# Score tiles of two PSUM banks for pairs of heads in a decoder step on one Trainium2 core

## The chip, the cores and the metric

The kernel runs on one core of a Trainium2 chip. The metric is the device time of one execution in microseconds (us), lower is better. TensorE is called PE below, VectorE DVE, ScalarE ACT, GpSimd POOL.

## The reference

The program is one step of a small hybrid decoder on 256 prompt tokens and 8 sample tokens (264 columns in all): an S5 layer with a gated projection, a squared-ReLU MLP, a sparse-attention layer with three branches (compressed, selected, window), and a second MLP. The attention of the prompt is, for each of 16 query heads over 4 key heads and a causal mask:

```python
s_s = einsum('bqgrd,bqgkld->bqgrkl', qg, ks)       # selected keys
p_s = _masked_softmax(s_s, sel_mask)
o_s = einsum('bqgrm,bqgmd->bqgrd', p_s, vs)
s_w = einsum('bqgrd,blgd->bqgrl', qg, kw)          # window keys
p_w = _masked_softmax(s_w, w_mask)
o_w = einsum('bqgrl,blgd->bqgrd', p_w, vw)
o = g[..., 0:1] * o_c + g[..., 1:2] * o_s + g[..., 2:3] * o_w
```

`o_c` is the same over 8 compressed blocks. With 256 tokens every causal block is selected, so both large branches are plain causal attention over 256 keys, each with keys and values of its own.

## The kernel before, in words

Activations lie feature-major, 128 features by 264 tokens. A dense product (`mm3`, L597 to L599) is three fp32r matmuls into one accumulator: high half of the weights by high half of the activations, high by low, low by high. The weights come by DMA into `raw` (four buffers) and `wsplit` makes the halves: ACT writes `wh` (L590), DVE subtracts and writes `wl` (L591).

The stages follow one another: S5 to about 127 us, gated projection and first MLP to 364, keys, values, gates and queries to 440, attention to 528, its output projection to about 552, second MLP to the end. The order of the S5 stage is written by hand (`tc.manual_schedule()`, L1484); that of everything else is set by the scheduler of the TileContext (L1725), engine by engine, from the program, the buffers of each pool and its own estimates. Each engine then runs its list in order.

The end of the S5 stage: `down(1, 8, 8)` multiplies and adds the last carries into the states `St` on DVE (L454, L455), `from_states` (L471) multiplies them on PE for feature tiles 6 and 7, and the gated projection begins. A `wl` of that projection's weights that the list puts between is run between. `filler` runs pieces of the sample's compression in the gaps of this stage.

PSUM has eight banks of 128x512 f32; a tile asked for with `K.ps(tag)` is one bank of a tag's buffers. Before, tags `fl` (2) and `tr` (3) live through the program, `mm` (3) until the first MLP is done, then `sc` (2) and `po` (1); from there on `mm` is another name for `fl`.

Keys on their way: `kv_post` (L950 on) brings a branch's keys token-major with four transposes (`token_major`, L934), norms and rotates them (`norm_rope`, L987 to L998, on ACT, DVE and POOL, with `rsqrt_bits` L128 to L137 in small steps on DVE), and turns them back into `KTp` (`feature_major`, L944, copy L945). `q_post` does it for queries into `QT`. The queries of head groups 0 and 1 (`gp` 0) are made before the attention begins, those of `gp` 1 partly beside it (`Q1`, and generator `side_a`).

Attention (`prompt_attn`) takes 12 units `(gp, rp, u)`, each for two head groups `g2`, whose queries and keys lie in partitions 0 to 63 and 64 to 127, one PSUM bank per `g2`. Unit `u` 0 has the first 128 tokens of two heads per group: a mask matmul over the whole bank (L1187), then score matmuls of 256 columns (L1191). Units `u` 1 and 2 have the other 128 tokens of one head: one score matmul of 512 columns per bank (L1195), then a mask matmul of 256 columns (L1198). Each f32 matmul with 64 partitions shows as passes in the trace. `softmax` takes the negated row maximum (L1212, DVE), exponentials with sums (L1214, ACT, 4 or 2 per bank), and the scale (L1215 to L1223). `transposed` turns the result with four transposes per bank (L1232), `values` multiplies with the values (L1246, L1253). The loop issues scores of unit i, softmax of unit i-1, transposes and values of unit i-2, then `side(i)`: as many steps as `SIDE[i]` of the remaining queries and the compressed branch (`cmp_branch`, L1156 on), and as `SIDB[i]` of the sample tokens' attention (`sample_qk`, `sample_attn`).

## Time and profile before

| what | value |
|---|---|
| runs | 742.78, 740.6, 740.55 us |
| median | 740.6 us |
| profiled execution | 741.12 us |
| its span | 739.3 us |
| mean granted PE clock | 0.975 of full speed |
| PE busy | 700.2 us (95%) |
| DVE busy | 531.7 us (72%) |
| ACT busy | 404.6 us (55%) |
| POOL busy | 74.8 us (10%) |

The span is the stretch from the first to the last instruction, 1.8 us shorter than the profiled execution's own time. Busy shares are averages over stages that differ, so they are read by stage in windows. A timeline lists the instructions of one engine in order with their start, and in brackets the idle time before one and what ended it. Durations of matmuls overlap the next one; the distance from start to start is what one costs.

### The profile page before, as it was taken

What the parts mean: (1) busy time and instruction counts of PE and PEld (TensorE: products, weight loads), DVE (VectorE), ACT (ScalarE), POOL (GpSimd) and SP (SyncE); (2) the same over time, 40 slices, a digit from 0 to 9 for tenths busy, and PEclk for the clock granted to TensorE, in tenths of its full rate; (3) what the DMA queues carried; (4) which work ended last, traced back from release to release, by engine and by line L of the source; (5) the groups of instructions that cost most, each with busy time, mean ns of one, the idle gap of its engine ahead of it and who ended that gap; (6) DMA issues with size and microseconds to landing.
All of it is one profiled execution on the core that took longest, in us unless ns stands there. A gap on an engine that the chain in (4) does not pass through costs nothing.

```text
span 739.3 us, 16322 instructions
## 1 busy us (share of the span) xinstructions
PE 700.2 (95%) x6214; PEld 650.7 (88%) x6214; DVE 531.7 (72%) x1209; ACT 404.6 (55%) x907; POOL 74.8 (10%) x127
## 2 busy tenths in 40 slices
PE   2789897999999999999998999999999999999997
PEld 2787777999999999999988984565899999999997
DVE  7899995978777766656677868887678777755553
ACT  3463532666666655445466575657466666644442
POOL 0000623111000000000002224110020000000000
PEclk9989897999999999999999996999999999999999
DMA  7342423686767758555555564100255555556551
GB/s 263 81 158 77 161 99 118 197 289 193 229 234 262 277 175 298 186 175 188 177 175 179 188 187 142 59 3 1 86 172 182 188 173 182 189 180 201 192 190 40
DMA packets 53328, 124.70 MB, mean 169 GB/s; under 512 B 6522, under 2 KB 26874, under 8 KB 52994
## 3 DMA queue, kind: packets, MB, share of 16 engines
q1 hardware_dynamic: 51714, 121.23, 49.9%
q10 hardware_dynamic: 1536, 2.42, 0.9%
q8 instruction: 49, 0.80, 0.5%
q14 instruction: 29, 0.24, 0.1%
HBM read 120.63 MB, written 7.18 MB: 173 GB/s over the span
## 4 chain that ended last, share of the span: by engine, by line
PE 83%; DVE 13%; ACT 2%; issue 1%; DMA 1%; SPq 0%; ACTq 0%; DVEq 0%
PE ps_mm L597 23%; PE ps_mm L598 22%; PE ps_mm L599 22%; PE ps_sc L1195 3%; PE ps_tr L296 2%; PE ps_tr L1232 2%; PE ps_po L1253 2%; DVE ca L431 1%; DVE St L434 1%; DVE St L433 1%; DVE cb L432 1%; DVE St L455 1%; DMA U<-x_chunks_in 1%; DVE big L454 1%; PE ps_sc L1198 1%
## 5 line engine op out<-in xcount | busy, mean ns | idle before, releaser
L591 DVE TENSOR_TENSOR wl<-raw,wh 128x512 fp32r<-128x512 f32 x344 | 241.1, 703 | 149.5 <-ACT wh L590 146.5
L590 ACT ACTIVATE wh<-raw 128x512 fp32r<-128x512 f32 x344 | 216.0, 631 | 210.7 <-PE ps_mm L598 157.8
L597 PE MATMUL ps_mm<-hh,wh 128*128 128x264 f32 x512 | 145.3, 284 | 0.0
L598 PE MATMUL ps_mm<-hl,wh 128*128 128x264 f32 x512 | 145.0, 283 | 0.0
L599 PE MATMUL ps_mm<-hh,wl 128*128 128x264 f32 x512 | 145.0, 283 | 0.0
L598 PEld LDWEIGHTS ps_mm<-hl,wh 128*128 128x128 f32 x512 | 96.5, 188 | 0.0
L597 PEld LDWEIGHTS ps_mm<-hh,wh 128*128 128x128 f32 x512 | 96.4, 188 | 0.0
L599 PEld LDWEIGHTS ps_mm<-hh,wl 128*128 128x128 f32 x512 | 96.0, 187 | 0.0
L598 PE MATMUL ps_mm<-yl,wh 128*128 128x264 f32 x256 | 72.9, 285 | 0.0
L597 PE MATMUL ps_mm<-yh,wh 128*128 128x264 f32 x256 | 72.6, 284 | 0.0
L597 PE MATMUL ps_mm<-xh,wh 128*128 128x264 f32 x256 | 72.6, 284 | 0.0
L599 PE MATMUL ps_mm<-yh,wl 128*128 128x264 f32 x256 | 72.5, 283 | 0.0
L598 PE MATMUL ps_mm<-xl,wh 128*128 128x264 f32 x256 | 72.4, 283 | 0.0
L599 PE MATMUL ps_mm<-xh,wl 128*128 128x264 f32 x256 | 72.3, 284 | 0.0
L597 PEld LDWEIGHTS ps_mm<-yh,wh 128*128 128x128 f32 x256 | 48.2, 188 | 0.0
L598 PEld LDWEIGHTS ps_mm<-xl,wh 128*128 128x128 f32 x256 | 48.2, 188 | 0.0
L597 PEld LDWEIGHTS ps_mm<-xh,wh 128*128 128x128 f32 x256 | 48.2, 188 | 0.0
L599 PEld LDWEIGHTS ps_mm<-yh,wl 128*128 128x128 f32 x256 | 48.2, 188 | 0.0
L598 PEld LDWEIGHTS ps_mm<-yl,wh 128*128 128x128 f32 x256 | 48.1, 188 | 0.0
L599 PEld LDWEIGHTS ps_mm<-xh,wl 128*128 128x128 f32 x256 | 47.9, 188 | 0.0
L628 POOL TENSOR_TENSOR nacc<-nacc,sq 128x264 f32<-128x264 f32 x21 | 16.9, 803 | 251.9 <-ACT sq L627 251.9
L598 PE MATMUL ps_mm<-gl,wh 128*128 128x264 f32 x128 | 36.6, 289 | 0.0
(424 smaller groups left out, 1482.3 us busy)
## 6 DMA issues: line engine op xcount, KB each, us to landing
raw<-w_up_in SPq DMA_DIRECT2D x64, 512.0 KB, 3.8
raw<-w_down_in SPq DMA_DIRECT2D x64, 512.0 KB, 3.6
raw<-s_w_glu_in SPq DMA_DIRECT2D x16, 512.0 KB, 4.8
w<-cmp_w_in SPq DMA_DIRECT2D x12, 512.0 KB, 4.5
raw<-w_kv_in SPq DMA_DIRECT2D x12, 512.0 KB, 3.5
blk<-cache_cmp_in SPq DMA_DIRECT2D x64, 64.0 KB, 1.9
raw<-w_q_in SPq DMA_DIRECT2D x8, 512.0 KB, 3.7
win_old_out<-cache_win_kv_in SPq DMA_DIRECT2D x8, 510.0 KB, 5.2
```

Source lines behind the costliest of these rows:

```text
L296: nc.tensor.matmul(pm[:, 0:73], sameT, sq[:, h, q, b], start=(h + q + b == 0), stop=(h + q + b == 9))
L431: TT(a, x, m(SR), ALU.mult)
L432: TT(b_, x[:, ::-1], m(SQ), ALU.mult)
L590: nc.scalar.activation(h[:, :, cols], src[:, c:c + 4], AF.Copy)
L591: nc.vector.tensor_tensor(l[:, :, cols], src[:, c:c + 4], h[:, :, cols].bitcast(F32), ALU.subtract)
L597: nc.tensor.matmul(out, wh, xh, start=start, stop=False)
L598: nc.tensor.matmul(out, wh, xl, start=False, stop=False)
L599: nc.tensor.matmul(out, wl, xh, start=False, stop=stop)
L628: nc.gpsimd.tensor_tensor(self.acc, self.acc, sq, ALU.add)
L1195: nc.tensor.matmul(banks[g2], K.QT[hs[g2], 4 * gp + 2 * rp + u - 1, 128:256], K.KTp[hs[g2], gp], start=True, stop=False)
L1232: nc.tensor.transpose(pt[:, 128 * j:128 * j + 128], Pf[:, 128 * j:128 * j + 128], K.ident)
L1253: nc.tensor.matmul(po[64 * g2:64 * g2 + 64, 128 * kt:256], K.Vp[:, kt, br, 64 * g:64 * g + 64], rhs, start=False, stop=(br == 1 and kt == 1))
```

## The change

- PSUM is shared out anew: `fl` 1 and `tr` 2 through the program, `mm` 4 and a new `fb` 1 until the first MLP is done, then two tiles `s2` of two banks each and `po` 1. `mm` becomes a rotation over tags: `fl`, `s2`, `s2` for the dense products outside the attention (an `s2` tile then gives its first bank), `fl` alone within it.
- `scores` takes one `s2` tile and uses its banks for the two head groups. `sample_attn` takes one for `p1` and `p2`, and its `pc` goes into unused columns of `po`.
- Token-major keys and values of the two large branches go to `tr` (before `sc`); `chunk_in`, the seventh `conv` and the compression in `filler` use other tags.
- A small exponential is put behind the gates' sigmoid on ACT, `cmp_branch(0)` stands behind the scores of unit 0, and `SIDE`, `SIDB` and `Q1` have other numbers.

```diff
-            pt = [ps("mm"), ps("tr")]
+            pt = [ps("mm"), ps("mm")]
...
-        pys[ft] = ps("mm" if ft < 7 else "tr")
+        pys[ft] = ps("mm")
...
-        pts = [K.ps("fl"), K.ps("fl")]
+        pts = [K.ps("fl"), K.ps("fb")]
...
-    pk = token_major(K, "sc", kv[:, 0:2])
+    pk = token_major(K, "tr", kv[:, 0:2])
...
-    pv = token_major(K, "sc", kv[:, 2:4])
+    pv = token_major(K, "tr", kv[:, 2:4])
...
     S.activation(g, g, AF.Sigmoid)
+    S.activation(ak.tile([1, 1], F32, name="tle"), g[0:1, 0:1], AF.Exp)
...
-        banks = [K.ps("sc"), K.ps("sc")]
+        pair = K.ps("s2")
+        banks = [pair[:, 0:512], pair[:, 512:1024]]
...
-    cmp_branch(0)
     for i in range(n + 2):
         if i < n:
             sc[i] = scores(*units[i])
+        if i == 0:
+            cmp_branch(0)
...
-        p1, p2 = K.ps("mm"), K.ps("mm")
+        pair = K.ps("s2")
+        p1, p2 = pair[:, 0:512], pair[:, 512:1024]
...
-        pc = K.ps("mm")
-        nc.tensor.matmul(pc[:, 0:64], ptx[:, 0], K.vcs[:, bh], start=True, stop=True)
+        pc = po[:, 256:320]
+        nc.tensor.matmul(pc, ptx[:, 0], K.vcs[:, bh], start=True, stop=True)
...
+    K.mm = ["mm"]
+
+    def ps(tag):
+
+        if tag == "mm":
+            tag = K.mm[0]
+            K.mm.append(K.mm.pop(0))
+            if tag == "s2":
+                return ps(tag)[:, 0:512]
+        pool, bufs, t = pools[tag]
+        return pool.tile([128, 1024 if tag == "s2" else 512], F32, tag=t, name="ps_" + tag, bufs=bufs)
+    K.ps = ps
...
-    pools["mm"] = pools["fl"]
+    wide = ["fl", "s2", "s2"]
+    K.mm = list(wide)
...
+            K.mm = ["fl"]
             prompt_attn(K, oh, ol, side)
...
+            K.mm = list(wide)
...
-PSC = dict(fl=2, tr=3)
-PSA = dict(mm=3)
-PSB = dict(sc=2,po=1)
-SIDE = (3,1,1,1,0,0,1,1,1,1,0,0,0,0)
-SIDB = (1,2,2,2,2,2,2,2,0,0,0,0,0,0)
-Q1 = 2
+PSC = dict(fl=1, tr=2)
+PSA = dict(mm=4, fb=1)
+PSB = dict(s2=2, po=1)
+SIDE = (1,1,1,2,2,2,1,1,1,1,0,0,0,0)
+SIDB = (0,0,0,1,2,2,2,2,2,2,2,0,0,0)
+Q1 = 1
```

What the scheduler makes of it, at three places. Line numbers of the changed kernel are one to three higher there (L1187, L1191, L1195, L1198, L1232 become L1189, L1193, L1197, L1200, L1234).

**PE, unit 4** (`gp` 0, `rp` 1, `u` 1), in the middle of the attention. `ps_sc` is a bank of scores, `ps_s2` a tile of two. Before:

```order
L1253 MATMUL ps_po_6450<-PT_6340,Vp_4951 64x128 x2
L1195 MATMUL ps_sc_6500<-KTp_4950,QT_4945 128x512
L1198 MATMUL ps_sc_6500<-triR_2872,identR_2874 128x2x128
L1195 MATMUL ps_sc_6501<-KTp_4950,QT_4945 128x512
L1198 MATMUL ps_sc_6501<-triR_2872,identR_2874 128x2x128
L1232 MATMUL ps_tr_6610<-ident_65,P_6508 128x128 x4
```

Now:

```order
L1248 MATMUL ps_po_6246<-pct_6031,vcm_5989 128x256
L1197 MATMUL ps_s2_6343<-KTp_4950,QT_4945 128x512 x2
L1200 MATMUL ps_s2_6343<-triR_2872,identR_2874 128x2x128 x2
L1255 MATMUL ps_po_6246<-PT_6156,Vp_4951 64x256
L1234 MATMUL ps_tr_6370<-ident_65,P_6218 128x128 x4
```

Before, the mask of one bank stands between the score matmuls of the two; now the two score matmuls stand together, then the two masks. All twelve units are in this form now; before, units 0 and 9 had the score matmuls of both banks together and the other ten had not.

**PE, from the last dense matmul to the first scores.** `ps_fl` and `ps_mm` are accumulators, `tm` is the token-major window keys after norm and rotation. Before (unit 0's score matmuls L1191 stand 32 rows further up, amid the dense work, and the transposes of `tm` into `ps_tr` 27 rows above those):

```order
L599 MATMUL ps_mm_6107<-qh_5278,wl_6125 128x264
L934 MATMUL ps_mm_6143<-ident_65,qr1_5939 128x128 x4
L1156 MATMUL ps_po_6034<-kcb_5976,QT_4945 128x16 x8
L1300 MATMUL ps_mm_6176<-ssq_6174,cst_64 128x96
L1195 MATMUL ps_sc_6221<-KTp_4950,QT_4945 128x512
L1198 MATMUL ps_sc_6221<-triR_2872,identR_2874 128x2x128
L1195 MATMUL ps_sc_6222<-KTp_4950,QT_4945 128x512
L1198 MATMUL ps_sc_6222<-triR_2872,identR_2874 128x2x128
L1195 MATMUL ps_sc_6316<-KTp_4950,QT_4945 128x512
L1198 MATMUL ps_sc_6316<-triR_2872,identR_2874 128x2x128
L1232 MATMUL ps_tr_6342<-ident_65,P_6229 128x128 x4
L1195 MATMUL ps_sc_6317<-KTp_4950,QT_4945 128x512
```

Now:

```order
L599 MATMUL ps_fl_6174<-qh_5278,wl_6192 128x264
L1075 MATMUL ps_po_5986<-vcp_5913,cst_64 64x64 x2
L934 MATMUL ps_fl_6259<-ident_65,qr1_5941 128x128 x4
L1157 MATMUL ps_po_6006<-kcb_5978,QT_4945 128x16 x8
L944 MATMUL ps_tr_5792<-ident_65,tm_5717 128x128 x4
L934 MATMUL ps_tr_5834<-ident_65,kv_5632 128x128 x4
L1101 MATMUL ps_tr_5891<-ident_65,gT_5885 128x48 x2
L1193 MATMUL ps_s2_5998<-KTp_4950,QT_4945 128x256 x4
L1197 MATMUL ps_s2_6070<-KTp_4950,QT_4945 128x512 x2
L1200 MATMUL ps_s2_6070<-triR_2872,identR_2874 128x2x128 x2
L1109 MATMUL ps_tr_5896<-cst_64,glt_5897 128x3
L974 MATMUL ps_tr_5904<-ident_65,kv_5632 8x128 x2
```

The transposes of the window keys, those of the window values and the gates, and unit 0's scores have moved behind the dense work; units 0 and 1 stand side by side and unit 2's scores follow six rows further down. The token-major transposes of the window keys, which before stood in front of the last 150 dense matmuls or so, now have only 48 dense matmuls behind them.

**DVE, the end of the S5 stage** (lines with + stand there now, with - before). `big` and `St` are the last product and sum of `down(1, 8, 8)`:

```order
 L454 TENSOR_TENSOR big_1431<-St1_637,sr_748 128x392
+L591 TENSOR_TENSOR wl_1658<-raw_1638,wh_1657 128x512
 L455 TENSOR_TENSOR St1_637<-St1_637,big_1431 128x8x7x7
+L454 TENSOR_TENSOR big_1434<-St1_637,sq_749 128x392
+L455 TENSOR_TENSOR St1_637<-St1_637,big_1434 128x8x7x7
 L591 TENSOR_TENSOR wl_1679<-raw_1675,wh_1678 128x512
 L591 TENSOR_TENSOR wl_1695<-raw_1675,wh_1694 128x512
-L454 TENSOR_TENSOR big_1434<-St1_637,sq_749 128x392
-L455 TENSOR_TENSOR St1_637<-St1_637,big_1434 128x8x7x7
```

The last product and sum have moved ahead of two of the four `wl`; of the other two, the one shown has moved down to stand behind the product `big_1431`.

## Rows read from the trace of the kernel before

**Rows 1.** The chain of work that ended last, by engine, on the page

```profile
PE 83%; DVE 13%; ACT 2%; issue 1%; DMA 1%; SPq 0%; ACTq 0%; DVEq 0%
```

**Rows 2.** Windows: us from:to, length, PE, PEld, DVE, ACT, POOL busy (instructions), PEclk, DMA share, GB/s

```profile
0.00:127.00 127.00, 97.02 (x1354) 88.66 (x1358) 110.03 (x274) 52.74 (x99) 25.65 (x52) 0.91 0.42 139
...
180.00:364.00 184.00, 184.00 (x1524) 184.00 (x1523) 121.63 (x216) 104.64 (x208) 6.68 (x13) 1.00 0.67 222
380.00:430.00 50.00, 47.31 (x408) 42.43 (x408) 40.91 (x112) 34.26 (x74) 14.21 (x13) 1.00 0.55 185
...
445.70:459.60 13.90, 13.90 (x30) 6.91 (x31) 11.09 (x48) 7.45 (x30) 7.30 (x13) 0.52 0.45 144
459.60:528.30 68.70, 68.59 (x503) 42.07 (x502) 52.06 (x161) 40.20 (x159) 6.93 (x15) 1.00 0.07 21
447.90:526.00 78.10, 77.99 (x510) 46.87 (x511) 60.35 (x199) 45.69 (x180) 13.40 (x28) 0.92 0.10 30
475.00:490.00 15.00, 15.00 (x93) 9.37 (x91) 14.20 (x48) 10.18 (x43) 1.57 (x1) 1.00 0.07 22
```

**Rows 3.** PE timeline, units 7 and 3: start, length, line, out<-in, shape, passes

```profile
481.60 1.12 PE L1195 MATMUL ps_sc<-KTp,QT 64*128 64x512 f32 x2
482.65 0.38 PE L1198 MATMUL ps_sc<-triR,identR 128*128 128x256 f32 x1
482.97 0.70 PE L1246 MATMUL ps_po<-pct,vcm 64*128 64x256 f32 x2
...
461.12 0.47 PE L1187 MATMUL ps_sc<-triR,identR 128*128 128x512 f32 x1
...
462.58 0.46 PE L1313 MATMUL ps_mm<-ssq,cst 128*128 128x96 f32 x2
```

**Rows 4.** PE timeline, unit 9, whose two banks stand together

```profile
495.34 0.73 PE L1187 MATMUL ps_sc<-triR,identR 128*128 128x512 f32 x2
495.91 0.38 PE L1232 MATMUL ps_tr<-ident,P 128*128 128x128 f32 x2
...
497.69 1.13 PE L1191 MATMUL ps_sc<-KTp,QT 64*128 64x256 f32 x8
498.76 0.55 PE L1232 MATMUL ps_tr<-ident,P 128*128 128x128 f32 x3
```

**Rows 5.** PE timeline, from the last dense work to unit 2

```profile
435.21 1.13 PE L1191 MATMUL ps_sc<-KTp,QT 64*128 64x256 f32 x8
...
440.92 0.60 PE L934 MATMUL ps_mm<-ident,qr 128*128 128x128 f32 x4
...
445.69 1.63 PE L1195 MATMUL ps_sc<-KTp,QT 64*128 64x512 f32 x2 [1.60 <-ACT P L1214]
...
455.64 0.58 PE L1198 MATMUL ps_sc<-triR,identR 128*128 128x256 f32 x1
```

**Rows 6.** DVE and ACT timelines, the window keys' way to KTp, and one step of rsqrt

```profile
417.52 0.67 DVE L988 TENSOR_REDUCE ss<-t 128x8 f32<-128x512 f32 x1
...
431.79 0.14 DVE L135 SCALAR_TENSOR_TENSOR rs<-rs,css 32x1 f32<-32x1 f32 x1
431.97 0.15 DVE L137 SCALAR_TENSOR_TENSOR rs<-rs,rs 32x1 f32<-32x1 f32 x1
...
431.29 0.60 ACT L945 ACTIVATE KTp<-ps_tr 128x512 f32<-128x512 f32 x1 [0.47 <-PE ps_tr L944]
```

**Rows 7.** DVE and ACT timelines, unit 0's maximum and its last exponential

```profile
441.65 1.27 DVE L1212 TENSOR_REDUCE nm<-ps_sc 128x4 f32<-128x512 f32 x2
...
446.54 0.40 ACT L1214 ACTIVATE P<-ps_sc,nm 128x128 f32<-128x128 f32 x1
```

**Rows 8.** DVE and PE timelines, the end of the S5 stage

```profile
110.21 1.39 DVE L591 TENSOR_TENSOR wl<-raw,wh 128x512 fp32r<-128x512 f32 x2
...
112.86 3.51 PE L471 MATMUL ps_mm<-St,Fb 128*32 128x72 f32 x120 [3.14 <-DVE St L455]
```

**Rows 9.** The window in which PE goes idle before unit 1; columns as in rows 2

```profile
444.00:445.00 1.00, 0.09 (x1) 0.00 (x0) 0.91 (x3) 0.99 (x6) 0.00 (x0) 1.00 0.98 301
```

More of the change, by code (lines that the diff above doesn't have):

```diff
@@ L1412, in sample_attn @@
         V.tensor_reduce(o, t.rearrange("p g d -> p d g"), AX.X, ALU.add)
-        V.tensor_tensor(o, o, pc[:, 0:64], ALU.add)
+        V.tensor_tensor(o, o, pc, ALU.add)
         yield
@@ L1461, in psum @@
             pools[tag] = pool, bufs[tag], tag
-    K.ps = lambda tag: pools[tag][0].tile([128, 512], F32, tag=pools[tag][2], name="ps_" + tag, bufs=pools[tag][1])
+    K.mm = ["mm"]
[8 more added lines that the diff above has]
+    K.ps = ps
     psum(ctx, "pc", PSC)
```

## The prediction

> **What bounds the kernel now.** I read the page's chain first. TensorE (PE) holds 83% of it and DVE 13% [rows 1], so time is to be won where PE is full, and DVE's share has to be found. The windows by stage show where [rows 2]. In the S5 stage (0 to 127 us) DVE is busy 110.03 of 127 us, 0.87, and PE waits. In the dense stages (180 to 364) PE is busy 184.00 of 184.00 us: PSUM buffers, weight splits and transfers are all covered there, and one matmul costs 184.00 / 1524 = 0.121 us. In the attention, 459.6 to 528.3, PE is busy 68.59 of 68.70 us at full clock. So there the time is PE's list of work, and each matmul that is saved counts, as long as DVE follows. DVE had 60.35 of the 78.1 us from 447.9 to 526, 77%; in the densest 15 us it had 14.20, 95%.
>
> Before that lies a bad stretch: PE goes idle (0.09 us busy in one, [rows 9]), unit 1's scores wait 1.60 us for unit 0's exponentials [rows 5], and then, 445.7 to 459.6, the granted clock is 0.52, the 1.2 GHz level, with PE busy all the time [rows 2].
>
> **The change part by part.** All terms are against the profiled execution, 741.1 us; its span is 739.3 and 1.8 lie around it. The median of the runs shown is 740.6, so 0.5 goes off at the end.
>
> *Pairs, -10.0.* With separate tiles unit 7 issues one bank: scores, mask, and the next work starts 482.97 - 481.60 = 1.37 us after it [rows 3]; two banks cost 2.74. Of that 1.05 (482.65 - 481.60) is the score matmul, which uses 64 partitions. Now the score matmuls of both banks stand next to each other, one on partitions 0 to 63, the other on 64 to 127. Unit 9 shows what that does: its eight passes over both banks take 498.76 - 497.69 = 1.07 us [rows 4], as long as the four of one bank elsewhere. The two run side by side. So a pair of unit 7's kind costs 1.05 for both scores, 0.32 for one mask (482.97 - 482.65), and 0.14 for the other (half of the 0.285 that a mask of twice the columns costs in unit 9, (495.91 - 495.34) / 2): 1.51, and saves 1.23. There are six such units behind 459.6 (4, 5, 7, 8, 10, 11): 7.4. Units 3 and 6 have the other form: a bank alone takes 462.58 - 461.12 = 1.46 [rows 3], two 2.92; together, as in unit 9, 0.57 + 1.07 = 1.64; twice 1.28 is 2.6. Units 0 and 9 were together already and give nothing. Bounds: if the mask after a pair costs as much as the first, 0.18 per unit less, so -8.9; nothing at all is a rival below.
>
> *The junction, -3.0.* Unit 0's scores need the window keys `KTp`, and these come later now. Their token-major transposes have 48 dense matmuls behind them, 48 x 0.121 = 5.8 us. The dense work ended at 440.92 [rows 5]; unit 0's scores (1.13) and two groups of four transposes (0.60 each) have gone from in front of that to behind it, so it ends near 438.6, and the chain starts near 432.8. How long it takes I bound from both sides. Before, its reduction began at 417.52 and its last copy ended at 431.29 + 0.60 [rows 6], 14.4 us, and transposes and square in front (0.60 each, by the transposes' row) make 15.6. The sum of its links with no wait is at least 0.60 + 0.60 + 0.67 + eleven rsqrt steps of 0.18 (431.97 - 431.79) + 0.60 + 0.60 = 5.1, POOL's passes not counted. I take the middle, 10.4, as the weight splits that it ran among end soon now: `KTp` at 443.2, unit 0's scores at 444.3, its maximum at 444.5 where it began at 441.65 [rows 7]: 2.9 late. Its exponentials ended at 446.94, so now at 449.8. That frees the first pair. Unit 1 waits for none of it, since it has the second pair; unit 2 follows at 449.8, and even at the low clock two times 1.51 plus a hand-over of 0.3 puts it at 453.1. Before, unit 2's second bank ended at 455.64 + 0.58 = 456.2 [rows 5]. That is 3 us won although unit 0 starts 8 us later than 435.21. Bounds: chain at 5.1, -5 to -6 (the queries and masks come next as limit); at 15.6, +2.
>
> *What DVE takes back, +4.6.* With 13 us of PE work gone, 65.1 us would hold DVE's unchanged 60.35: 93% of the time. DVE's work comes in hand-overs (PE, maximum, ACT, scale, PE), and the stage of this kernel that DVE sets, S5, reaches 0.87 [rows 2]. At that pace the stretch takes 60.35 / 0.866 = 69.7, so 8.4 of the 13.0 are kept. Bounds: 0 back (93% is under the 95% of 475 to 490), or 8.7 back at the 0.82 of the stretch 380 to 430 (40.91 / 50), which is the pace with more waits. The single accumulator `fl` of the sample's and the queries' steps, and the sample's use of a pair, which leaves one for the prompt until its exponentials are done, are waits of this kind and inside these bounds; they are spread between units, and PE's other work (transposes, values) lies between.
>
> *The end of S5, -1.3.* PE waits 3.14 us there for the last `St` [rows 8]. Two `wl`, 1.39 by their row (about 1.3 from start to start), stood in front of it on DVE and now follow it. They are needed only by the gated projection, after 3.51 us of PE work. Bounds: 0, if the sum's input is late from elsewhere, to -1.8, if the one that moved behind `big_1431` also counts.
>
> *Costed at nothing.* The early exponential brings the table load ahead on ACT: the maximum of unit 0 runs beside it either way. `chunk_in`, the seventh `conv`, `filler` and two `tr` buffers in S5: DVE, not a PSUM tile, ends PE's waits there. Four `mm` buffers instead of three, and three banks in rotation instead of two in the second MLP: PE is at 184.00 of 184.00 in the dense stretch. `pc` in `po`'s bank: it is written and read behind `po` anyway. If the covers fail, the cost is in the range.
>
> Sum: -10.0 - 3.0 + 4.6 - 1.3 = -9.7; 741.1 - 9.7 = 731.4; less 0.5, **730.9 us**.
>
> **A rule against the trace.** The rows above give DVE 77% with PE full, and I let it rise to 87%. The Trainium skill, page "TensorEngine Tiling (Array Packing)", section "PSUM Bottleneck", says that tiling makes TensorE faster but not the evacuation of PSUM, which may become the bound. By that rule none of the gain beyond DVE's present pace is safe; the trace so far agrees that DVE has little room (the 95% above), and does not show which pace it can hold.
>
> **The rivals.**
>
> 1. *DVE's hand-overs hold at 0.82.* For it: each unit is a chain over three engines, and waits for `fl` and for a pair add to it; against it: the 95% of 475 to 490. Then the stretch takes 60.35 / 0.818 = 73.8, a gain of 4.3, with S5's 1.3 it is 735.5, less 0.5: **735.0**. In the changed profile PE would show waits for DVE in nearly every unit. This is where the skill's rule would lead.
>
> 2. *The low clock does not come.* If PE is kept busy across the junction, the 13.9 us at 0.52 would be done in 7.2, 6.7 less. DVE must then do 95%: 60.35 / 0.947 = 63.7, a gain of 14.4, with S5 725.4, less 0.5: **724.9**. For it: units 0 and 1 no longer wait on each other. Against it: `KTp` comes at about 443, some 4 us after the dense work, with little for PE between.
>
> 3. *Slower: more low clock.* Before, one idle spell was followed by 13.9 us at 0.52, a loss of 6.7. The forecast itself has PE waiting 4.6 us in the attention, which had 0.1. If two more spells like that follow from such waits, they cost 13.4: 730.9 + 13.4 = **744.3**. It decides from about 9.7 / 6.7 = 1.4 further spells. For it: PE has no slack work once it is ahead of DVE. Against: waits inside a unit are parts of a us, where the one before 445.7 was over 1.5.
>
> 4. *No side by side.* The eight passes of unit 9 are 64x256, the pairs now 64x512 with one pass after the other per bank; if the order within the pair did not let them overlap, only junction and S5 remain, -4.3: **736.3**.
>
> 5. *No change.* The gain is lost to waits for `fl`, pairs and the later keys: **740.6**, within 2.
>
> **How the numbers follow.** Forecast 0.52, rival 1 0.15, rival 2 0.12, rival 4 0.05: these are faster, 0.84. Rival 5 0.07 is "same" (0.3%, 2.2 us, is about what a measurement of this kernel can tell from no change). Rival 3 0.09 is slower. The range leaves out rivals 3 and 5 and takes in the others, and with them the bounds on DVE's pace, the junction and S5: 724.0 to 737.5.
>
> **What would show it.** In the changed profile: the two score matmuls of a pair as one group of four passes in about 1.1 us, and a pair with masks in about 1.5; six units later PE ahead and waiting on DVE's maximum or scale, DVE at about 87% of an attention of some 70 us; unit 0's scores near 443 and unit 2's done near 453; PE's wait at the end of S5 nearer 1.8 than 3.14 us; the dense stages unchanged. Wrong it would be if the pairs take 2.7 us, if the granted clock is low in places where it was full, if PE waits in the dense stages for PSUM, or if DVE is full there at less than 80%.

## The result and the profile after

The change makes the kernel slower: 749.0 us median (four runs, 745.65 to 750.3) against 740.6 of the kernel before in the same comparison (737.6 to 742.8), a ratio of 1.011 with a 95% interval of 1.0061 to 1.0158. The forecast was 730.9. The profiled execution took 748.75, its span 747.0. One execution of a kernel can be some per cent longer than another, at a lower granted clock: the ratios below are of the shorter ones alone, and the profiles of e10, x5_narrow and x5_fl are of longer ones, so that their low clock is an upper figure.

The chain of the changed kernel, by engine, to be held against [rows 1]: PE has lost 8 points, DVE, ACT, DMA and POOL have won them.

```profile
PE 75%; DVE 16%; ACT 4%; DMA 2%; issue 1%; POOL 1%; SPq 0%; ACTq 0%; DVEq 0%; POOLq 0%
```

Windows of the changed kernel, columns as in [rows 2]: the dense stretch; then from its first key product to the first product of the second MLP, whole and by stage (rest of the dense products, junction, body of the attention, output projection).

```profile
180.00:364.00 184.00, 184.00 (x1520) 184.00 (x1520) 123.12 (x233) 104.39 (x210) 6.68 (x13) 1.00 0.66 222
360.40:556.50 196.10, 179.44 (x1384) 144.73 (x1384) 145.18 (x414) 115.99 (x343) 32.37 (x53) 0.95 0.36 117
422.60:443.20 20.60, 18.10 (x145) 16.95 (x143) 16.56 (x59) 13.74 (x29) 4.84 (x4) 1.00 0.22 70
443.20:464.00 20.80, 15.04 (x72) 10.69 (x72) 16.08 (x53) 9.28 (x36) 9.58 (x17) 0.67 0.26 90
464.00:525.80 61.80, 56.45 (x442) 34.60 (x441) 48.45 (x159) 38.89 (x163) 4.54 (x15) 0.97 0.22 70
525.80:556.50 30.70, 30.63 (x241) 27.71 (x242) 21.45 (x41) 16.99 (x39) 4.34 (x6) 1.00 0.38 121
```

The same stages of the kernel before:

```profile
358.80:548.80 190.00, 185.25 (x1384) 144.84 (x1383) 144.16 (x415) 117.64 (x342) 36.54 (x53) 0.96 0.37 121
419.90:440.90 21.00, 21.00 (x170) 19.27 (x169) 14.82 (x53) 14.13 (x32) 5.45 (x5) 1.00 0.55 174
440.90:459.60 18.70, 16.75 (x54) 9.39 (x53) 15.13 (x56) 11.99 (x43) 7.84 (x14) 0.64 0.56 173
459.60:523.10 63.50, 63.39 (x461) 37.80 (x460) 49.39 (x156) 38.55 (x156) 6.93 (x15) 1.00 0.06 18
```

Before the first key product the change loses 1.6 us (360.4 against 358.8), from there to the second MLP 6.1 (196.1 against 190.0); the second MLP takes 190.5 us in both. The 1.6 us are not clear of noise: the first key product starts at 354.9 to 360.5 us in the changed kernel and in e1, e4, e8 and x4, whose edits all lie behind it, and at 354.5 to 359.4 in the kernel before and in e2, e3, e10 and e12. I split that middle stretch in three: idle of PE (length less PE busy), the share lost to the low clock (PE busy times one less the granted clock, window by window of 1 us), and the rest, PE's work at full clock.

| middle stretch, us | length | PE idle | lost to low clock | PE work |
|---|---|---|---|---|
| before | 190.0 | 4.8 | 6.8 | 178.4 |
| after | 196.1 | 16.6 | 8.4 | 171.1 |

PE does 7.3 us less work. It idles 11.8 us more.

Where the idle time lies shows when the stretch is cut at the end of unit 2's scores (456.2 before, 463.4 now). Both parts hold as many matmuls as before, 701 and 685. Before, then now:

```profile
358.80:456.20 97.40, 92.76 (x701) 79.33 (x700) 73.19 (x215) 61.47 (x148) 22.01 (x27) 0.95 0.57 186
456.20:548.80 92.60, 92.49 (x685) 65.50 (x684) 70.97 (x202) 56.17 (x194) 14.53 (x27) 0.98 0.17 53
```

```profile
360.40:463.40 103.00, 91.76 (x701) 81.81 (x701) 74.68 (x216) 59.50 (x141) 22.89 (x33) 0.92 0.43 145
463.40:556.50 93.10, 87.68 (x685) 62.92 (x684) 70.49 (x199) 56.49 (x203) 9.48 (x21) 0.98 0.27 86
```

The first part is 5.6 us longer, with 6.6 us more idle time (103.00 - 91.76 against 97.40 - 92.76). The second is 0.5 us longer: PE is busy 4.8 us less and idles 5.3 us more.

PE's timeline of the changed kernel at the junction, to be held against [rows 5], and a pair with its masks further on, against [rows 3]. The transposes at 435.24 begin the way of the window keys to `KTp`:

```profile
435.24 0.60 PE L934 MATMUL ps_tr<-ident,kv 128*128 128x128 f32 x4
...
439.73 0.39 PE L597 MATMUL ps_fl<-qh,wh 128*128 128x264 f32 x1 [0.93 <-ACT qr L1125]
...
449.88 0.79 PE L1193 MATMUL ps_s<-KTp,QT 64*128 64x256 f32 x1
...
454.22 0.38 PE L1109 MATMUL ps_tr<-cst,glt 48*128 48x3 f32 x2
...
460.56 2.08 PE L1197 MATMUL ps_s<-KTp,QT 64*128 64x512 f32 x4 [3.83 <-ACT P L1216]
462.57 0.79 PE L1200 MATMUL ps_s<-triR,identR 128*128 128x256 f32 x2
...
469.63 1.13 PE L1197 MATMUL ps_s<-KTp,QT 64*128 64x512 f32 x4
470.69 0.50 PE L1200 MATMUL ps_s<-triR,identR 128*128 128x256 f32 x2
471.12 0.65 PE L1255 MATMUL ps_po<-PT,Vp 128*64 128x256 f32 x2
```

A pair now costs 471.12 - 469.63 = 1.49 us. But ACT's copy into `KTp` ends at 449.7:

```profile
449.12 0.60 ACT L945 ACTIVATE KTp<-ps_tr 128x512 f32<-128x512 f32 x1 [3.45 <-PE ps_tr L944]
```

So unit 0's scores start at 449.9, where the forecast had 443, and then unit 2 waits 3.83 us for unit 0's exponentials and ends at 463.4, not 453. DVE's timeline shows why the exponentials are late, to be held against [rows 7]:

```profile
448.65 1.12 DVE L133 TENSOR_TENSOR rs<-rs 128x8 f32<-128x8 f32 x1
449.80 0.17 DVE L135 SCALAR_TENSOR_TENSOR rs<-rs,ss 128x8 f32<-128x8 f32 x1
...
454.64 0.28 DVE L1107 TENSOR_TENSOR glt<-gT,cst 48x128 f32<-48x128 f32 x1 [2.93 <-PE ps_tr L1109]
455.75 0.29 DVE L1159 TENSOR_TENSOR cS<-ps_po,cst 128x128 f32<-128x128 f32 x1 [0.83 <-PE ps_tr L1109]
455.96 0.68 DVE L1214 TENSOR_REDUCE nm<-ps_s 128x4 f32<-128x512 f32 x1
```

Unit 0's scores are done by about 452.2 (eight passes from 449.88 to 450.11 + 2.04). Its maximum (L1214) stands in DVE's list behind `glt`, a product for the sample's gates, and behind a product of the compressed branch (L1159). `glt` has one buffer and waits 2.93 us for the L1109 matmuls that read it; these stand on PE behind unit 1's pair, and that pair runs at the low clock (the junction's granted clock is 0.67 in the windows). The product behind `glt` waits another 0.83 us. So the maximum starts at 455.96, almost 4 us late. No run moves `glt` alone, so what these 4 us cost in the end is not tested.

The end of S5 in the changed kernel, DVE and PE timelines, against [rows 8]:

```profile
111.36 1.28 DVE L591 TENSOR_TENSOR wl<-raw,wh 128x512 fp32r<-128x512 f32 x2
...
114.93 0.62 PE L795 MATMUL ps_fb<-blk,w 128*128 128x272 f32 x2
115.48 2.08 PE L471 MATMUL ps_mm<-St,Fb 128*32 128x72 f32 x128
117.49 0.39 PE L597 MATMUL ps_mm<-gh,wh 128*128 128x264 f32 x1
```

The wait of 3.14 us is gone. PE fills it with sample compression (L795), moved from elsewhere, and reaches the gated projection at 117.49 instead of 116.30. That difference too is inside what executions vary by (113.6 to 117.5 in the changed kernel and e1, e4, e8, x4; 114.4 to 116.3 in the kernel before and e2, e3, e10, e12). A last part of the compression, by the groups of the first MLP's up part, now stands where PE is full and where the kernel before had none:

```profile
L817 PE MATMUL ps_fl<-w,chid 128*128 128x64 f32 x8 | 1.0, 268 | 0.0
```

### The profile page after: what moved, and what is told of

Its sections match the earlier page's. It is cut to its first block, busy times and chain, and to the rows that moved or that the text cites. A ratio compares the mean times of both kernels' runs of the same rounds, so it can differ in the third digit from the quotient of the medians.

```text
span 747.0 us, 16327 instructions
## 1 busy us (share of the span) xinstructions
PE 697.8 (93%) x6214; PEld 651.8 (87%) x6214; DVE 532.7 (71%) x1209; ACT 403.1 (54%) x908; POOL 69.9 (9%) x127
## 4 chain that ended last, share of the span: by engine, by line
PE 75%; DVE 16%; ACT 4%; DMA 2%; issue 1%; POOL 1%; SPq 0%; ACTq 0%; DVEq 0%; POOLq 0%
PE ps_mm L598 10%; PE ps_mm L597 10%; PE ps_mm L599 10%; PE ps_s L597 8%; PE ps_s L598 8%; PE ps_s L599 8%; PE ps_fl L597 4%; PE ps_fl L598 4%; PE ps_fl L599 4%; PE ps_tr L296 2%; PE ps_po L1255 1%; DVE ca L431 1%; DVE St L434 1%; DVE St L433 1%; DVE big L454 1%
## 5 line engine op out<-in xcount | busy, mean ns | idle before, releaser
L597 PE MATMUL ps_mm<-hh,wh 128*128 128x264 f32 x256 | 72.6, 284 | 0.0
L597 PE MATMUL ps_mm<-xh,wh 128*128 128x264 f32 x256 | 72.6, 284 | 0.0
L598 PE MATMUL ps_mm<-hl,wh 128*128 128x264 f32 x256 | 72.5, 283 | 0.0
L599 PE MATMUL ps_mm<-hh,wl 128*128 128x264 f32 x256 | 72.5, 283 | 0.0
L597 PE MATMUL ps_s<-hh,wh 128*128 128x264 f32 x192 | 54.5, 284 | 0.0
L598 PE MATMUL ps_s<-hl,wh 128*128 128x264 f32 x192 | 54.4, 283 | 0.0
L599 PE MATMUL ps_s<-hh,wl 128*128 128x264 f32 x192 | 54.4, 283 | 0.0
L597 PEld LDWEIGHTS ps_mm<-xh,wh 128*128 128x128 f32 x256 | 48.2, 188 | 0.0
L598 PEld LDWEIGHTS ps_mm<-hl,wh 128*128 128x128 f32 x256 | 48.2, 188 | 0.0
L597 PEld LDWEIGHTS ps_mm<-hh,wh 128*128 128x128 f32 x256 | 48.2, 188 | 0.0
L599 PEld LDWEIGHTS ps_mm<-hh,wl 128*128 128x128 f32 x256 | 48.0, 187 | 0.0
L598 PE MATMUL ps_s<-yl,wh 128*128 128x264 f32 x168 | 47.8, 285 | 0.0
L597 PE MATMUL ps_s<-yh,wh 128*128 128x264 f32 x168 | 47.6, 283 | 0.0
L628 POOL TENSOR_TENSOR nacc<-nacc,sq 128x264 f32<-128x264 f32 x21 | 16.3, 777 | 244.4 <-ACT sq L627 244.4
```

Of the source, the lines that this page charges most:

```text
L597: nc.tensor.matmul(out, wh, xh, start=start, stop=False)
L598: nc.tensor.matmul(out, wh, xl, start=False, stop=False)
L599: nc.tensor.matmul(out, wl, xh, start=False, stop=stop)
L628: nc.gpsimd.tensor_tensor(self.acc, self.acc, sq, ALU.add)
```

## The experiments

All are timed against the kernel before on the same chip. The ratios with their intervals, and the middle stretch as above:

| kernel | ratio to before | length | idle | low clock | work |
|---|---|---|---|---|---|
| after | 1.011 [1.006, 1.016] | 196.1 | 16.6 | 8.4 | 171.1 |
| e1_keys_off_tr | 1.018 [1.009, 1.027] | 204.1 | 21.1 | 12.0 | 171.0 |
| e2_before_keys_on_tr | 1.020 [1.010, 1.030] | 208.7 | 8.7 | 22.1 | 177.9 |
| e3_before_pair_only | 1.009 [1.004, 1.013] | 197.2 | 17.2 | 9.0 | 171.0 |
| e4_no_early_exp | 1.006 [1.001, 1.011] | 193.7 | 16.2 | 6.3 | 171.2 |
| e5_before_psum_until_attention | 1.008 [1.003, 1.014] | 196.3 | 16.8 | 10.3 | 169.3 |
| e6_same_no_early_exp | 1.010 [1.005, 1.014] | 199.7 | 17.0 | 13.8 | 169.0 |
| e7_same_no_exp_old_tables | 1.012 [1.004, 1.020] | 198.0 | 17.5 | 9.3 | 171.2 |
| e8_change_with_old_tables | 1.015 [1.006, 1.025] | 202.8 | 18.2 | 10.8 | 173.8 |
| e9_no_exp_copies_on_act | 1.005 [1.001, 1.009] | 193.6 | 15.4 | 6.3 | 171.9 |
| e10_before_copies_on_act | 0.999 [0.994, 1.005] | 199.0 | 4.7 | 16.0 | 178.3 |
| e11_no_exp_no_scale | 1.004 [1.001, 1.008] | 192.5 | 14.6 | 7.7 | 170.1 |
| e12_before_no_scale | 1.005 [1.000, 1.009] | 200.0 | 4.6 | 16.1 | 179.3 |
| x4_single | 1.028 [1.020, 1.036] | 208.6 | 9.5 | 18.5 | 180.6 |
| x5_narrow | 1.021 [1.015, 1.027] | 212.0 | 11.3 | 21.8 | 178.9 |
| x5_fl | 1.027 [1.018, 1.037] | 227.5 | 12.1 | 38.2 | 177.1 |
| x5_tr | 1.009 [1.005, 1.012] | 195.7 | 5.2 | 11.9 | 178.6 |
| y1_two_accumulators | 1.043 [1.040, 1.045] | 212.0 | 26.8 | 11.3 | 173.9 |
| y2_sample_on_fl_and_tr | 1.034 [1.030, 1.037] | 213.3 | 23.6 | 16.3 | 173.4 |

The column of the low clock is of one execution each, and it varies without any change of PSUM: e10 and e12, which only take work off DVE, show 16 us of it against 6.8 before. A cost is therefore read from the ratios, and the low clock is named as its form only where all executions of a kernel agree: the mean granted clock was 0.957 to 0.966 in all four of x4 and 0.938 to 0.966 in all four of x5_fl, while in the kernel before, timed beside them, it was 0.975 to 0.981 in six of seven.

**First: single parts undone or done alone.** My first theory was that unit 0's keys, which now come late by way of `tr`, cost the time; the rivals were the two-bank tile and the early table load.

```diff
e1 (after)   token_major(K, "tr", ...) -> token_major(K, "mm", ...), keys and values
e2 (before)  token_major(K, "sc", ...) -> token_major(K, "tr", ...), keys and values
e3 (before)  banks = [K.ps("sc"), K.ps("sc")] -> the halves of one K.ps("s2"), PSB = dict(s2=1, po=1), keys and values in its first bank
e4 (after)   the exponential behind the gates' sigmoid taken out
```

> The changed kernel, with the token-major keys and values of the two large branches taken from the rotation of fl and the two-bank tiles instead of the two tr tiles. Theory K (the loss is made at the junction: keys that wait for one of two tr tiles come late, KTp at 449.7 us, and PE idles 8.3 us between 422 and 464): unit 0's scores come back to 434 to 440 us, PE's idle time at the junction falls by about 6 us, the total to 739 to 743 us. Rival E (the early exponential's table load in front of weight splits on ACT): keys earlier, but PE still stops for the splits, total within 2 us of 749. Rival D (the attention's hand-overs and the single accumulator fl set the end): unit 0 earlier, but the last unit is not, total 746 to 750.

> The kernel before, with this one edit of the change: token-major keys and values of the two large branches on tr (three tiles there). Theory K: the keys come behind the dense work here too, unit 0's scores move from 435 to 446 to 450 us and the total rises by 5 to 9 us, to 746 to 750. Rivals E and D: this edit is not the cause, 739 to 742 us.

> The kernel before, with one tile of two banks for the scores of a unit (no second one), all else as before, the token-major keys in the first bank of that tile. The pairs are put to the test alone: the score matmuls of a unit should take 1.5 instead of 2.7 us, so PE's work is 8 to 10 us less. With one tile each unit's scores wait for the last exponential of the unit before. If those waits cost less than the pairs give (theory K has the pairs as a gain): 734 to 738 us. If hand-overs take back all (rival D): 740 to 745 us, with PE idle 8 us or more in the attention.

> The changed kernel without the small exponential behind the gates' sigmoid. Theory K: the keys stay late, total 747 to 750 us. Rival E: the table load of 1.28 us and the waits it causes on PE at 432 to 434 us are gone, total 744 to 746 us.

e1 brings the first scores back to 438.5 (83.6 us after its first key product; 76.4 before, 89.5 after), but its stretch is longer, 204.1. PE's table of waits in e1 (engine, line, for whom: us in total, times, longest) shows a new stall at the sample's sums, whose input is late and which stand in front of other work in PE's list, and, earlier in the stretch (428.75), a wait for the accumulator to be read:

```profile
PE ps_fl L1316 <- DVE ssq L1314: 6.6, 1, 6.6
PE ps_fl L597 <- ACT qr L1125: 2.8, 1, 2.8
```

So in the kernel with pairs the late keys are not what binds: the theory fell. Yet e2 shows that putting them on `tr` costs the kernel before 2.0%, in its profile for the most part by 15.3 us more at the low clock. e3, with one pair tile, has the same saving of work (171.0) and as much idle as the change, 17.2; it takes no bank from another tag, and its time of 749.0 us lies above both ranges that were expected. So the gain is lost without the narrow sharing too. e4's point of ratio, 1.006, lies under the change's 1.011; the intervals overlap, and the stretch is 2.4 shorter. ACT's timeline of the changed kernel shows three table loads of 1.28 us within 5 us, where the order puts another function (L1052) between the sigmoid and the exponential. Their number is the same without the early exponential (e4: 426.54, 428.27 and 453.52); the edit only brings the third one forward, ahead of weight splits. In e4 PE's wait of 1.57 us for the queries' rotation at 434.75 is gone; that the load caused it fits, but is not shown.

```profile
426.43 1.28 ACT L1096 ACT_TABLE_LOAD   x1
...
428.17 1.28 ACT L1052 ACT_TABLE_LOAD   x1
...
429.77 1.28 ACT L1097 ACT_TABLE_LOAD   x1
```

**Second: the sharing before the attention, and the order tables.**

```diff
e5 (after)  until the attention fl, fx, tr, tr, tx and sc (2) as before; then fl 1, tr 2, s2 2
e6          e5 without the early exponential
e7          e6 with SIDE, SIDB and Q1 of before
e8 (after)  SIDE, SIDB and Q1 of before
```

> The changed kernel, with PSUM shared as before until the queries of the first group are made (two accumulators, three tr, two single banks for token-major keys and values) and the two-bank tiles made only for the attention; order tables and early exponential as in the change. Theory K2 (the loss is made before the attention, by late keys and by one accumulator for queries, not by the pairs): first scores 76 to 80 us after the first key product instead of 89.5, and from that product to the second MLP 184 to 190 us instead of 196.1, total 736 to 743 us. Rival D (the attention's own hand-overs with two tiles set the end, whatever the start): 192 to 198 us for that stretch, total 745 to 750.

> As the run before (PSUM as before until the attention) and also without the early exponential. If the table load in front of the weight splits costs what it showed in the changed kernel (2.4 us of the stretch from first key product to second MLP): 182 to 188 us for that stretch, total 734 to 741 us. If it is covered here: the same as the run before, within 1 us of the stretch.

> As the run before, and with the order tables of the kernel before (queries of the second group and the sample's steps earlier). Theory T (the changed tables crowd DVE and POOL in the middle of the attention): the stretch gets shorter by 2 us or more. Theory K2 alone: tables are worth less than 2 us either way.

> The changed kernel with the order tables of the kernel before and nothing else. Theory K2: keys stay late (first scores 88 us or more after the first key product), the stretch from first key product to second MLP stays at 194 to 198 us, total 747 to 751. Theory T: the stretch falls under 192 us.

None is faster than the change beyond its interval; idle stays at 17 to 18. e5 brings unit 0's scores back to 77.6 us after the first key product, and its stretch is still 196.3 us, as the rival had it: PE then waits 4.0 us for exponentials at a later unit. Neither the sharing ahead of the attention nor the tables explain it.

**Third: less work for DVE.** If DVE's throughput set the pace, PE's idle should fall by what is taken from DVE. e11 and e12 leave out the scale of the late units' probabilities.

```diff
e9 (after, no early exponential, S5 tiles of before)  CPA = (0,) -> CPA = (0, 1)   both PT copies on ACT
e10 (before)                                          CPA = (0,) -> CPA = (0, 1)
e11 (as e9, CPA = (0,))   else: V.tensor_tensor(P, ...) -> elif u == 0: V.tensor_tensor(P, ...)
e12 (before)              the same
```

> The changed kernel without the early exponential, with the S5 stage's PSUM tiles as before (three mm, three tr; chunk_in and the seventh conv on tr), and with both copies of the transposed probabilities of the late units on ACT (before one of the two on DVE: 8 copies of 0.60 us, 4.8 us off DVE). First part, up to the first key product: if the 1.3 us in the first MLP come from sample compression moved into it by those tiles, it is 357.5 to 359.5 long and not 360.4. Second part, first key product to second MLP, 193.7 us without this (idle 16.2). Theory DVE (in the pair kernels DVE's queue sets the pace, so work off DVE shortens PE's idle time): 188 to 191 us, idle 11 to 14. Rival chain (the latency of the hand-overs sets the pace, whichever engine copies): within 1.5 us of 193.7. Rival clock (idle time is only where the order puts it; the low clock decides): unchanged idle, the rest as the granted clock goes.

> The kernel before with both copies of the transposed probabilities of the late units on ACT and nothing else. Theory DVE: PE is the bound there (idle 4.8 us in the same stretch of 190.0), so the 4.8 us off DVE give less than 1.5 us. If it gains 3 us or more, DVE set the pace before too, and the pairs could give nothing from the start.

> As the run with both copies on ACT, but with the copies as they were, and the multiplication of the exponentials of the late units (u 1 and 2) by gate over sum is left out: the probabilities of those units are not scaled. That takes 16 DVE instructions of about 0.6 us, 9.6 us, and one hand-over per bank out. Theory DVE: the stretch falls by 5 to 9 us, to 185 to 189, idle to 8 to 11. Rival chain: it falls too, as one hand-over of each unit is gone, but by 2 to 4 us. Rival clock: under 2 us unless the granted clock rises.

> The kernel before with the same multiplication left out (probabilities of the late units not scaled). Theory DVE with PE the bound before: the stretch of 190.0 falls by less than 3 us, as only 4.8 us of it are idle on PE. Rival (DVE sets the pace in both): it falls by 5 us or more, as in the pair kernel.

The middle stretch of e4, e9 and e11, one row each, columns as above (the third number with a count is DVE):

```profile
360.50:554.20 193.70, 177.46 (x1385) 143.57 (x1384) 144.52 (x414) 115.78 (x342) 32.17 (x53) 0.96 0.37 119
```

```profile
356.50:550.10 193.60, 178.24 (x1384) 143.71 (x1383) 138.82 (x407) 119.44 (x350) 32.32 (x53) 0.96 0.36 119
```

```profile
359.20:551.70 192.50, 177.85 (x1385) 144.15 (x1384) 135.69 (x399) 116.63 (x342) 32.83 (x53) 0.96 0.37 120
```

Against e4, e9 takes 5.7 us from DVE and idle falls by 0.8; e11 takes 8.8 and idle falls by 1.6. How much DVE has to do is not what holds PE. The order and the length of single hand-overs remain as the explanation; the timeline at the junction shows one, and no run changes one alone. In the kernel before, the same two edits gain nothing (0.999 and 1.005) and leave its idle at 4.6 to 4.7. The first part of e9 came to 356.5 us and that of e11, which is the same up to there, to 359.2: this part varies by more than the range that was expected of it, 357.5 to 359.5, which so decides nothing. The last of the compression stands in the first MLP's time in both, so the S5 tiles of the change did not move it there.

**Fourth: tiles and sharing taken apart.** In the attention all eight banks are taken, before (`fl` 2, `tr` 3, `sc` 2, `po` 1) and after (`fl` 1, `tr` 2, two `s2` of two, `po` 1): the two extra banks of the pairs come from one accumulator and one transpose buffer. These four runs separate the pair from that price.

```diff
x4 (after, no early exponential)  pair = K.ps("s2") -> K.ps("sc"), K.ps("sc"); PSB = dict(sc=4, po=1); wide = ["fl", "sc", "sc"]
x5_narrow (before)  from prompt_attn on mm and fl have one buffer, tr two (the third ones lie unused)
x5_fl (before)      only the accumulator so
x5_tr (before)      only tr so
```

> The change without the early exponential, and with four score tiles of one bank (tag sc) where it has two of two banks; everything else (one fl, two tr, mm in rotation, order) as in the change. Three theories of why PE idles 15 to 21 us between the first key product and the second MLP in every kernel with pairs so far (4.8 before). (A) The coarse tile: a pair is only handed over and freed as a whole. Then idle falls to 5 to 8 here although the accumulators stay narrow, PE's work is back at 174 to 178, and the stretch takes 187 to 192. (B) The narrow sharing (one accumulator, two tr buffers): idle stays at 13 to 18. (C) The scheduler's order, whatever the tiles: idle changes in no foreseeable way, and the waits lie at other lines.

> The kernel before, with one accumulator and two tr buffers while the attention runs, as the change has them; score tiles of one bank as before. (A) coarse tile: idle of PE in the stretch stays near 4.8, the stretch at 190 to 192, time the same as before within 0.4%. (B) narrow sharing: idle rises to 10 to 15, the stretch to 195 to 202, the time by 1 to 1.5%. (C) order: PE waits at places that neither the accumulator nor tr explains.

> The kernel before, with one accumulator and the three tr buffers while the attention runs. If (B) holds by the accumulator, this has the idle of x5_narrow; if by tr, this has 5 to 6 and the time of before. (A): 5 in all of them.

> The kernel before, with two tr buffers and the two accumulators while the attention runs. If (B) holds by tr, this has the idle of x5_narrow; if by the accumulator, 5 to 6 and the time of before. (A): 5 in all of them.

x4 is the change without its pairs (and without the early exponential; the scheduler still puts the score matmuls of units 0 and 1 together); e4 is the same with them. x4: the whole stretch, and a window at the junction:

```profile
354.90:563.50 208.60, 199.12 (x1384) 152.50 (x1383) 146.80 (x415) 117.78 (x342) 33.87 (x53) 0.91 0.35 111
...
460.00:468.00 8.00, 8.00 (x24) 4.83 (x23) 3.93 (x11) 4.38 (x19) 0.76 (x3) 0.50 0.01 2
```

From before to x4 the time grows by 2.8%, 0.0277 x 739.3 = 20 us: that is everything in the change but pairs and exponential, the late keys and the tables included. From x4 to e4 it falls to 1.0058 / 1.0277 = 0.979, some 16 us: that is what the pairs are worth on top of it, and the two intervals don't meet. By the table the pairs take 9.4 us of work away, add 6.7 of idle, and end with 12.2 less at the low clock.

x5_fl shows one large part of the price: with one accumulator in place of two the kernel before is 2.7% slower; x5_narrow, with the narrow `tr` too, is 2.1% slower, the same within the intervals; x5_tr alone 0.9%. (All three also give the buffers two names each; that alone was not run, and x5_tr bounds it.) The late keys alone, e2, cost 2.0%, so the accumulator is not shown to be the larger of the two. PE's waits in x5_fl, of which the kernel before has only the one for `P`, once [rows 5]:

```profile
PE ps_fl L1416 <- DVE so L1413: 1.6, 2, 1.3
PE ps_fl L944 <- POOL qn L998: 1.6, 1, 1.6
PE ps_sc L1195 <- ACT P L1214: 1.5, 3, 1.0
PE ps_fl L597 <- ACT oh L606: 1.1, 1, 1.1
PE ps_fl L1400 <- ACT QT L945: 0.7, 1, 0.7
PE ps_fl L597 <- ACT qr L1124: 0.6, 1, 0.6
```

Two of them are for the accumulator itself, to be read by ACT (`QT` at L1400 and `qr` at L597, 0.7 + 0.6 = 1.3 us); `so`, `qn` and `oh` are inputs (1.6 + 1.6 + 1.1 = 4.3) that PE meets too early in the order that was written around one accumulator. Together that is 5.6 of the 7.3 us by which idle rises. In the changed kernel the accumulator's wait is there as well, 0.93 at 439.73 in the timeline above, but the larger ones are at the pairs. So (B), narrow sharing, holds as a price, in x4 and x5_fl more by the low clock than by the idle itself; (A), the coarse tile, fell as the cause of the loss, though pairs go with most of the idle in the change (6.7 of 11.4 us in e4). x4's 9.5 us of idle lie between what (A) and (B) had expected, 5 to 8 and 13 to 18. Over all runs, every kernel with pairs idles 14.6 us or more in this stretch, whatever its accumulators, `tr` buffers, tables and work on DVE, and every kernel without them 12.1 or less.

**Last: could the price be avoided within eight banks?**

```diff
y1 (after, no early exponential)  PSC = dict(fl=1, tr=2) -> dict(fl=2, tr=1)
y2 (after, no early exponential)  in the attention K.mm = ["fl"] -> ["fl", "tr"]
```

> The change without the early exponential, with two accumulators fl and one tr buffer, where the change has one and two; pairs as in the change. In the kernel before, one accumulator in place of two added 6 to 7 us of idle PE and 15 to 31 us at the low clock. (B) If that is also what eats the gain of the pairs in the change, idle falls from 16 to about 10, the stretch from 193.7 to 184 to 188, the time to 732 to 738, under that of before; one tr buffer costs a little of it (two in place of three cost 0.4 of idle). (A) If the coarse tile is the main cause, idle stays at 14 to 17 and the time at 743 to 750.

> The change without the early exponential; while the attention runs, what takes mm (queries, sample, projections) alternates between the one fl and the two tr buffers instead of taking fl alone; pairs as in the change. (B) The waits for fl go (0.9, 0.6, 0.5, 0.4, 0.2 by the table of waits), some of them come back at tr; idle falls from 16 to 11 to 13, the stretch to 188 to 191, the time to 738 to 743. (A) idle stays at 14 to 17 and the time at 743 to 750.

Both are much slower than the change; the hope for a faster version fell. In y1, with all transposes on one `tr` buffer, PE waits 6.59 us for POOL's rotation of a key tile, with no other work ahead of it, and 4.67 for a copy of `PT` out of `tr`:

```profile
460.72 1.12 PE L944 MATMUL ps_tr<-ident,tm 128*128 128x128 f32 x4 [6.59 <-POOL tm L998]
...
491.75 2.82 PE L1254 MATMUL ps_po<-PT,Vp 128*64 128x256 f32 x14 [4.67 <-DVE PT L1243]
```

In y2 the waits are spread, and two lie at `tr`, where the sample's steps now stand among the transposes. That the second accumulator would repay its bank in the change is not shown; a ninth bank, which would tell, does not exist.

```profile
PE ps_fl L944 <- POOL qn L998: 3.1, 1, 3.1
...
PE ps_tr L1403 <- ACT ptx L1399: 2.2, 1, 2.2
PE ps_tr L1233 <- DVE t L993: 2.0, 1, 2.0
```

## Why the prediction was wrong

The profiled executions lie 748.75 - 741.12 = 7.6 us apart, where the sum had -9.7. By part, in us:

| part | forecast | measured | missed by |
|---|---|---|---|
| up to the first key product (end of S5) | -1.3 | +1.6 | 2.9 |
| from there to the end of unit 2 (junction) | -3.0 | +5.6 | 8.6 |
| from there to the second MLP (pairs and what DVE takes back) | -10.0 + 4.6 = -5.4 | +0.5 | 5.9 |

**Junction, -3.0: the step that failed.** The chain of `KTp` began at 435.2 instead of 432.8 and took to 449.7, 14.5 us, close to its upper bound of 15.6, where I took the middle. Unit 2 ended at 463.4, 7.2 later than before, which is beyond the bound of +2: that bound counted the chain alone, not that unit 0's maximum would stand in DVE's list behind an operation that waits for PE, almost 4 us. Junction and the dense rest in front of it (422.6 to 464.0) have 8.3 us of idle against 1.95 in 419.9 to 459.6 before. In the kernel before, late keys alone (e2) cost 2.0%, where this term had a gain; yet e5 shows that early keys alone don't bring the gain back.

**"What DVE takes back, +4.6": near in size by luck, wrong in its reasons.** Behind unit 2 PE idles 5.3 us more. But the term let DVE rise from 77% to 87%. In the body of the attention DVE did 48.45 of 61.80 us, 78%, and before 49.39 of 63.50, 78%: it kept its share, under the 82% of rival 1, and PE, with less to do, idled 5.35 us where it had 0.11. e9 and e11 show that this is no limit on DVE's throughput. The Trainium skill, page "TensorEngine Tiling (Array Packing)", section "PSUM Bottleneck", says that the copying out of PSUM may become the bound when tiling speeds up TensorE. The runs agree only in part: the gain beyond DVE's present pace was not safe, but 5.7 and 8.8 us less work on DVE took only 0.8 and 1.6 us off PE's idle.

The term also put the single accumulator among waits "inside these bounds". Alone, in the kernel before, it costs 2.7%, 20 us, twice the pairs' term; the bound of 8.7 was set by a pace of DVE, and a wait for a buffer is not bounded by that. The changed kernel itself waits 0.9 us for the accumulator to be read; how much of the 20 us its order holds otherwise is not shown. The Trainium skill, page "TensorEngine Tiling (Array Packing)", section "Gotcha 1: PSUM Pressure", says that row tiles write to different PSUM banks and so press on PSUM; that is the price that I left out, and x5_narrow and x5_fl put 2 to 3% on it here.

**Pairs, -10.0: the price right, the sum too large.** 1.49 us for a pair against 1.51 worked out; rival 4 is out. But PE's work fell by 7.3 us from before to after, by 7.4 in e3 and by 9.4 from x4 to e4, where ten pairs at the worked-out saving, eight in this term and two under the junction, make some 12. Where the rest went I have not traced.

**End of S5, -1.3: not seen.** The wait went as said, but PE's list there had been filled with sample compression, and 1.0 of it stands in the full first MLP. In these two profiles the gated projection starts 1.2 later; neither a gain nor a loss is clear of what executions vary by.

**"Costed at nothing": partly wrong.** The early exponential comes to about 2.4 us by the stretch of e4, not resolved by the ratios; two `tr` for three to 0.9%. The bank of `pc` and the rotation show nothing: the second MLP is the same to 0.1 us.

**Rivals.** Slower was given 0.09, by more low clock. The changed kernel has only 1.6 us more of it; its loss is idle. The low clock is the form that the same price takes in x4 and x5_fl, and in e2's profile.

What stays open: why spells of idle bring the low clock for 14 us in one execution (before, 445.8 to 459.8) and for 56 in another (x5_fl), which of the late keys, the accumulator and the tables makes how much of x4's price, and why single edits of e1, e5 and y2 move the stalls elsewhere instead of removing them. Each edit also makes the scheduler write another order, so the parts don't add up (2.7, 2.0 and 0.9% alone, 2.8% together).

## What to carry to other kernels

When a larger PSUM tile saves matmul time, cost the banks it takes from other tags as a term of its own, by removing them from the kernel before and nothing else; here those runs would have turned the forecast (15 to 20 us against a gain of 9.7). A buffer count at which PE never waits says nothing of the count below it. And where an engine runs its list in order, look for what stands in front of the instruction that others wait for: a maximum of 0.7 us came almost 4 us late behind a small product for another purpose. Before a difference of 1 or 2 us in a stage is explained, look what that stage takes in other kernels that share it: here up to 5.6 us more or less.

## What the runs showed of the hardware

The granted clock stayed at the lower of its two levels (1.2 and 2.4 GHz) although PE was busy without a gap. In x4 that lasted at least 24 us, 452 to 476 (the row of 460 to 468 stands above). In the profiled execution of x5_fl, its longest, it was 56 us, after three waits of 0.27 to 0.96 us between 445 and 450, and the clock came back in a window in which PE idles:

```profile
444.00:452.00 8.00, 6.18 (x22) 3.09 (x20) 7.68 (x27) 5.93 (x22) 1.27 (x1) 0.91 0.81 274
452.00:508.00 56.00, 56.00 (x175) 29.52 (x174) 30.24 (x93) 19.57 (x80) 10.17 (x26) 0.50 0.07 20
508.00:516.00 8.00, 5.93 (x44) 4.06 (x42) 4.57 (x19) 4.06 (x14) 1.04 (x1) 0.93 0.00 0
```

A product of 128x8 on DVE took 1.12 us in place of 0.17 (448.65 in DVE's timeline above) and ended at 449.77, when POOL's product of 512 columns ended (448.48 + 1.27 = 449.75):

```profile
448.48 1.27 POOL L995 TENSOR_TENSOR qn<-qn,t 128x512 f32<-128x512 f32 x1 [1.36 <-DVE rs L128]
```

The Trainium skill, page "SBUF — State Buffer", section "Who interferes with whom", has a rule for it: a DVE instruction with two inputs from SBUF contends with a POOL instruction that reads SBUF. The trace agrees here with its times, POOL having begun first.
